# GLA scores in two row halves of the TensorE array, two heads each, into two PSUM banks

## The chip, the cores and the metric

One core of a Trainium2 chip runs the kernel. The metric is the device time of one execution in microseconds (us); the time before is the median of three runs. The engines are TensorE (PE, with its weight loads shown apart as PEld), VectorE (DVE), ScalarE (ACT), GpSimd (POOL) and SyncE (SP), which issues most of the DMAs.

## The reference, cut to what matters

Two layers of a backbone over 1024 latent tokens and 256 context tokens of width 1024. Each layer normalises and modulates the tokens, projects them, and gives the columns to four mixers (gated linear attention, neighbourhood attention, S5, pooling); their gated outputs are projected back and added. The change lies in the gated linear attention (GLA): four heads with keys and queries of 32 elements and values of 64, run forward and backward over the tokens.

```python
def step(state, inp):
    qc, kc, vc, gc = inp
    b = jnp.cumsum(gc, axis=-2)
    diff = b[:, :, :, None, :] - b[:, :, None, :, :]
    decay = jnp.exp(jnp.where(lower[:, :, None], diff, -jnp.inf))
    att = jnp.einsum('bhid,bhjd,bhijd->bhij', qc, kc, decay)
    o = (jnp.einsum('bhij,bhje->bhie', att, vc)
         + jnp.einsum('bhid,bhde->bhie', qc * jnp.exp(b), state))
    ...
o = (gla_chunked(qh, kh, vh, log_gate(gf, 0), s_f)
     + flip_seq(gla_chunked(flip_seq(qh), flip_seq(kh), flip_seq(vh), flip_seq(log_gate(gb, 1)), s_b)))
y = gla_head_norm(o, g_norm)
```

## The kernel before, in words

All 1280 tokens are cut into ten chunks of 128. Keys and queries of the four heads lie on the 128 partitions (32 per head), tokens along the free axis: QF and KF for the forward direction, QB and KB for the backward one, already multiplied with the exponentials of the gates.

A layer goes through stages: the GLA projections, then a stage in which GLA runs beside the projections of S5 and of the neighbourhood attention and beside the modulation, then S5, pooling, the neighbourhood attention and the output projection. `gla` (L978) is the GLA stage. Its preparation (`gla_prep`, L864, and L986 to L1012) makes the gates' running sums by scans, the four operands (L1002 to L1006), and a maximum over the gates (L1008), which PE transposes (L1010) and VectorE reduces to a flag; the flag chooses a general path, not taken here. A backward loop (L1049) builds the states of the backward direction for all chunks into `glSb`.

The forward loop (L1053 to L1073) then takes the chunks in order. For each chunk that is kept (ten in layer 0; eight in layer 1, where the context gives no output) and each direction:

- `gla_spread` copies the chunk's queries four times, each copy with the rows of one head kept and the others zero, into `qs` (128 x 512): by four ScalarE instructions (L971) forward, by one GpSimd instruction (L973) backward, as the string BD says.
- One fp32 matmul (L1062) with the keys as weights on all 128 rows and `qs` as the moving operand gives the scores of four heads, 128 x 512, in one PSUM bank of the pool `pb`.
- VectorE masks them into `at`: the forward direction by a multiplication (L1065), the backward one by a predicated copy over it (L1067). There are two `at` buffers (ATB).

`gla_finish` then sums into a `pb` bank: the forward state (L946, weights QF, moving operand `Sft`, made by VectorE at L1040), the masked scores times the values (L948, four heads), the backward state (L950). ScalarE squares the sums (L953), VectorE reduces the squares (L955), takes the reciprocal root in eleven small steps (L132 to L140) and multiplies (L957), PE transposes the result (L960), ScalarE writes `glyst` (L962) and it is stored. The forward state moves on by `state`: a transpose of the keys (L934), a copy by ScalarE (L936), a matmul (L938), two VectorE instructions (L1031, L1032).

PSUM in this stage: two banks for the projections (`pa`), one for the modulation (`pm`), five for GLA (`pb`; npb, L1536).

The order of instructions on every engine is set when the program is built, by a scheduler that takes GLA's instructions first and fills the gaps that it expects with the other mixers' projections (L318 with 512 columns, L334 with 256 columns, both into `pa`; their sums go on to `stn` and `stg` by L1200 and L1219 on VectorE) and with the modulation (L198 on 32 columns of the array, L229). Each engine then runs its list strictly in that order. In the trace an fp32 matmul of GLA appears as two instructions of the same columns.

## Time and profile before

| what | value |
|---|---|
| median of three runs | 1439.78 us (1434.55 to 1441.52) |
| the profiled execution's own time | 1441.78 us |
| its span | 1440.0 us |
| PE busy | 1286.8 us (89%) |
| DVE busy | 898.0 us (62%) |
| ACT busy | 585.0 us (41%) |
| POOL busy | 414.0 us (29%) |

The profile comes from one execution. The shares of busy time are means over stages with different limits, so the stretches and the waits in them tell more than the table.

### The profile page before, as it was taken

To read this page: it belongs to the slowest core of one execution; us is meant where nothing else is said; L and a number is where in the kernel's file an instruction comes from. 1 tells how busy PE (TensorE), PEld (TensorE's weight loads), DVE (VectorE), ACT (ScalarE), POOL (GpSimd) and SP (SyncE) were. 2 spreads that over 40 slices of the span, in tenths; PEclk is the share of its full clock that TensorE was granted. 3 is DMA by queue.
4 is the path that set the end of the run, shared out by engine and by line. 5 is a ranking of instruction groups with operands and counts; after the bars stand their busy time and mean duration, and the time that the engine had idled before them with its cause. 6 is when DMAs were issued, how large, how long until landed. Compare 5 with 4: busy or idle time off the path is not lost. (4 is left out here: it accounts for less than half of the span.)

```text
span 1440.0 us, 20173 instructions
## 1 busy us (share of the span) xinstructions
PE 1286.8 (89%) x6958; PEld 1025.7 (71%) x6958; DVE 898.0 (62%) x2113; ACT 585.0 (41%) x1218; POOL 414.0 (29%) x368
## 2 busy tenths in 40 slices
PE   5798988999999899989999898888989989977897
PEld 2687956567777688767778877856867766765676
DVE  2878576555378557844654578385553894776473
ACT  2642433222333346733455642442233323665321
POOL 0215342010101033432654536331121110234351
PEclk9798999999999999989999998989999999988999
DMA  9445674762533277726842374655324535755662
GB/s 333 144 125 182 210 214 137 211 178 64 178 116 115 91 202 179 208 87 210 241 130 92 113 215 163 205 169 143 107 77 158 156 125 150 196 158 163 180 205 90
DMA packets 223479, 231.09 MB, mean 160 GB/s; under 512 B 47016, under 2 KB 176552, under 8 KB 223040
## 3 DMA queue, kind: packets, MB, share of 16 engines
q1 hardware_dynamic: 221776, 227.14, 52.3%
q10 hardware_dynamic: 1584, 2.49, 0.5%
q8 instruction: 59, 0.97, 0.3%
q14 instruction: 60, 0.49, 0.1%
HBM read 159.97 MB, written 69.62 MB: 159 GB/s over the span
## 5 line engine op out<-in xcount | busy, mean ns | idle before, releaser
L303 POOL TENSOR_TENSOR wl<-w,wh 128x1024 fp32r<-128x1024 f32 (+1 forms) x45 | 118.1, 2632 | 437.6 <-PE pa L318 197.1
L318 PE MATMUL pa<-ahi,wh 128*128 128x512 f32 (+1 forms) x664 | 175.2, 392 | 5.5 <-DVE stg L856 2.5
L318 PE MATMUL pa<-ahi,wl 128*128 128x512 f32 (+1 forms) x664 | 171.1, 385 | 0.4 <-PEq L1555 0.4
L318 PE MATMUL pa<-alo,wh 128*128 128x512 f32 (+1 forms) x664 | 168.2, 380 | 0.1
L318 PEld LDWEIGHTS pa<-ahi,wh 128*128 128x128 f32 x664 | 119.2, 198 | 34.5 <-issue 8.4
L318 PEld LDWEIGHTS pa<-ahi,wl 128*128 128x128 f32 x664 | 117.1, 195 | 28.9 <-issue 11.3
L318 PEld LDWEIGHTS pa<-alo,wh 128*128 128x128 f32 x664 | 115.8, 194 | 25.5 <-issue 7.5
L334 PE MATMUL pa<-wh,ahi 128*128 128x256 f32 (+1 forms) x480 | 84.8, 311 | 6.3 <-ACT wh L302 2.4
L388 PE MATMUL po<-wx,ahi 128*128 128x512 f32 x312 | 82.8, 407 | 4.8 <-ACT ahi L380 2.6
L334 PE MATMUL pa<-wl,ahi 128*128 128x256 f32 (+1 forms) x480 | 81.5, 304 | 2.5 <-POOL wl L303 2.5
L334 PEld LDWEIGHTS pa<-wh,ahi 128*128 128x128 f32 x480 | 70.2, 201 | 14.2 <-issue 5.4
L334 PE MATMUL pa<-wh,alo 128*128 128x256 f32 (+1 forms) x480 | 78.2, 300 | 0.0
L302 ACT CAST wh<-w 128x1024 fp32r<-128x1024 f32 (+1 forms) x51 | 53.7, 1056 | 57.3 <-PE pa L318 34.9
L1315 PE MATMUL nS<-naK,naQ 128*128 128x256 f32 (+2 forms) x256 | 58.8, 349 | 19.8 <-DVE nast L1322 17.3
L388 PEld LDWEIGHTS po<-wx,ahi 128*128 128x128 f32 x312 | 61.1, 197 | 19.5 <-ACT ahi L380 3.5
L334 PEld LDWEIGHTS pa<-wl,ahi 128*128 128x128 f32 x480 | 69.2, 199 | 5.8 <-POOL wl L303 3.0
L334 PEld LDWEIGHTS pa<-wh,alo 128*128 128x128 f32 x480 | 67.9, 197 | 1.7 <-issue 1.4
L1322 DVE CUSTOM_DVE_ANT_0 naP<-nS,nab 128x640 f32<-128x640 f32 (+1 forms) x64 | 50.2, 785 | 28.9 <-ACT nab L1273 14.8
L1315 PEld LDWEIGHTS nS<-naK,naQ 128*128 128x128 f32 x256 | 45.0, 204 | 32.0 <-DVE nast L1322 26.2
L198 PE MATMUL pm<-wm,csil 128*32 128x512 f32 x192 | 47.8, 679 | 19.0 <-DVE nr2v L132 9.5
L973 POOL TENSOR_TENSOR qs<-QB,ind 128x512 f32<-128x512 f32 x18 | 18.8, 1047 | 148.4 <-PE pb L1062 144.3
L1327 ACT ACTIVATE naP<-naP,nast 128x640 f32<-128x640 f32 (+1 forms) x64 | 51.5, 804 | 22.8 <-DVE nast L1322 17.5
(395 smaller groups left out, 2735.2 us busy)
## 6 DMA issues: line engine op xcount, KB each, us to landing
wm<-in_w_mod_dram SPq DMA_DIRECT2D x48, 512.0 KB
w<-in_w_in_dram SPq DMA_DIRECT2D x41, 512.0 KB
s5R<-dR SPq DMA_DIRECT2D x16, 960.0 KB
xt<-in_tok_dram SPq DMA_DIRECT2D x20, 512.0 KB
dR<-sp_R SPq DMA_DIRECT2D x16, 512.0 KB
dG<-stg SPq DMA_DIRECT2D x32, 256.0 KB
w<-in_w_out_dram SPq DMA_DIRECT2D x16, 512.0 KB
naQ<-dQ SPq DMA_DIRECT2D x24, 320.0 KB
```

The source lines that it names most:

```text
L198: nc.tensor.matmul(state[0][32 * k:32 * k + 32, :], lhsT=self.csil[:, (k0 + k) // 2, 2 * (k % 2):2 * (k % 2) + 32], rhs=ws[k // 2][:, k % ...
L302: nc.scalar.copy(hi, raw)
L303: (next(engines) if engines else self.eng(2)).tensor_tensor(lo, raw, hi.bitcast(F32), ALU.subtract)
L318: nc.tensor.matmul(ps[:, :t1 - t0], lhsT=w(k), rhs=x[:, k, t0:t1], start=(i == 0), stop=(i == 23))
L334: nc.tensor.matmul(ps[:, :n], lhsT=x[:, k, t * 128:(t + 1) * 128], rhs=w(k), start=(i == 0), stop=(i == 23))
L388: self.nc.tensor.matmul(o, lhsT=x[:, k], rhs=m(k), start=first and i == 0, stop=last and i == len(todo) - 1)
L973: (nc.gpsimd if BD[d] == "p" else nc.vector).tensor_tensor(out, Q.unsqueeze(1).to_broadcast(sh), ind.unsqueeze(2).to_broadcast(sh), ALU.mult)
L1315: nc.tensor.matmul(ps[:, c * 128:(c + n) * 128], lhsT=Qb[:, i, :], rhs=K[:, b * 128:(b + n) * 128], start=(i == 0), stop=(i == 1))
L1322: v.tensor_tensor_reduce(P[:, 0:nk], ps, bias[:, b0:b0 + nk], 1.0, -NEG, ALU.add, ALU.min, nm)
L1327: nc.scalar.activation(P[:, 0:nk], src, AF.Exp, bias=nm, scale=-1.0, accum_out=l1)
```

## The change

The queries are spread to even and odd heads only. One copy keeps the rows of heads 0 and 2, the other those of heads 1 and 3 (`ind1` becomes 128 x 2), so `qs` has 128 x 256 elements; ScalarE makes both copies in both directions. The scores of a direction come from two matmuls: rows 0 to 63 of keys and `qs` (heads 0 and 1), and rows 64 to 127 (heads 2 and 3), 256 columns each. The two halves write into two PSUM banks: one tile `sc` of 1024 columns holds both directions of both halves of a chunk, and there is one such tile. The masks read it through a four-dimensional view. The pool `pb` goes from five banks to three.

```diff
--- before.py
+++ after.py
@@ -48,7 +48,6 @@
 WO = 0
 PO = ((4, 4, 'naK'), (0, 2, 'naQ'))
 OE = -2
-BD = 'ap'
 ATB = 2
 QSB = 2
 SLO = '11111111'
@@ -962,15 +961,10 @@
         nc.scalar.activation(yst, pt[:, 0:256].rearrange("p (m i) -> p m i", m=2), AF.Copy, scale=gn)
         self.q(1).dma_start(self.dY[l][0:256, c * 128:(c + 1) * 128].rearrange("(m p) i -> p m i", p=128), yst)
 
-    def gla_spread(self, out, Q, ind, d):
-
-        nc = self.nc
-        sh = [128, 4, 128]
-        if BD[d] == "a":
-            for h in range(4):
-                nc.scalar.activation(out[:, h], Q, AF.Copy, scale=ind[:, h:h + 1])
-        else:
-            (nc.gpsimd if BD[d] == "p" else nc.vector).tensor_tensor(out, Q.unsqueeze(1).to_broadcast(sh), ind.unsqueeze(2).to_broadcast(sh), ALU.mult)
+    def gla_spread(self, out, Q, ind):
+
+        for h in range(2):
+            self.nc.scalar.activation(out[:, h], Q, AF.Copy, scale=ind[:, h:h + 1])
 
     BWD = [1, 0] + list(range(NT - 1, 1, -1))
 
@@ -1015,7 +1009,7 @@
                 bm, gn = self.gla_consts(l)
                 mf = self.t([128, 128], "mF", 1)
                 nc.sync.dma_start(mf, a["maskF"])
-                ind = self.t([128, 4], "ind1", 1)
+                ind = self.t([128, 2], "ind1", 1)
                 nc.sync.dma_start(ind, a["ind1"])
                 mb = self.t([128, 128], "mB", 1, dtype=I32)
                 nc.sync.dma_start(mb, a["maskB"])
@@ -1054,17 +1048,21 @@
                     vt = self.gla_load_v(l, c)
                     if not (last and c < 2):
                         at = self.t([128, 4, 128], "at", ATB)
-                        sh = [128, 4, 128]
+
+                        ps = self.ps2.tile([128, 1024], F32, tag="sc", bufs=1, name=self.nm("sc"))
+                        pd = ps.rearrange("p (b d n) -> p d b n", b=2, d=2)
                         for d, (K, Q) in enumerate(((KF, QF), (KB, QB))):
-                            qs = self.t(sh, "qs", QSB)
-                            self.gla_spread(qs, Q[:, cs], ind, d)
-                            ps = self.pb()
-                            nc.tensor.matmul(ps, lhsT=K[:, cs], rhs=qs.rearrange("p h i -> p (h i)"), start=True, stop=True)
-                            pv = ps.rearrange("p (h i) -> p h i", h=4)
-                            if d == 0:
-                                v.tensor_tensor(at, pv, mf.unsqueeze(1).to_broadcast(sh), ALU.mult)
-                            else:
-                                v.copy_predicated(at, mb.unsqueeze(1).to_broadcast(sh), pv)
+                            qs = self.t([128, 2, 128], "qs", QSB)
+                            self.gla_spread(qs, Q[:, cs], ind)
+                            for b in range(2):
+                                hp = slice(64 * b, 64 * b + 64)
+                                nc.tensor.matmul(pd[:, d, b], lhsT=K[hp, cs], rhs=qs[hp].rearrange("p h i -> p (h i)"), start=True, stop=True)
+                        av = at.rearrange("p (b h) i -> p b h i", b=2)
+                        sh = [128, 2, 2, 128]
+                        every = lambda m: m.unsqueeze(1).unsqueeze(1).to_broadcast(sh)
+                        pv = pd.rearrange("p d b (h i) -> p d b h i", h=2)
+                        v.tensor_tensor(av, pv[:, 0], every(mf), ALU.mult)
+                        v.copy_predicated(av, every(mb), pv[:, 1])
                         sf = turned(S, 0, c, self.t([128, 256], "Sft", 2))
                         self.gla_finish(l, c, vt, lambda h: at[:, h, :], QF[:, cs], sf, QB[:, cs], Sb[:, c, :], gn)
                     if c != NT - 1:
@@ -1533,7 +1531,7 @@
                 psum = self.ps2
                 pm = lambda: psum.tile([128, 512], F32, tag="pm", bufs=1, name=self.nm("pm"))
                 todo = ((1, (2,)),) if last else ((0, (2,)), (1, (1, 0)))
-                self.npb = 5
+                self.npb = 3
                 flag = self.gla(l, last)
                 self.npb = 6
                 raws = itertools.cycle([("wm", 3, pool)])
@@ -1612,7 +1610,7 @@
     for h in range(4):
         ind[32 * h:32 * h + 32, h] = 2.0
     out["ind2"] = ind
-    out["ind1"] = (ind > 0).astype(f)
+    out["ind1"] = (ind[:, 0:2] + ind[:, 2:4] > 0).astype(f)
     lm = np.zeros((128, 5, 32), np.int32)
     j = np.arange(128)[:, None] % 32
     i = np.arange(32)[None]
```

Three lines come out of the changed file, so its numbers are lower: the score matmuls are L1059, L946, L948, L950, L955, L957 and L960 are L945, L947, L949, L954, L956 and L959, the masks are L1064 and L1065, L1040 is L1034, L1008 and L1010 are L1002 and L1004, L996 and L997 are L990 and L991, L1002, L1005 and L1006 are L996, L999 and L1000, L1031 and L1032 are L1025 and L1026, L318 and L334 are L317 and L333, L1200 and L1219 are L1198 and L1217.

The scheduler gives the instructions other places. PE, forward loop of layer 0, from the scores of one chunk to the transposes of another, before (`pa` is a projection's bank, `wh` and `wl` its weights, `ahi` and `alo` its tokens):

```order
L1062 MATMUL pb_2080<-qs_2075,KF_1561 128x512
L1062 MATMUL pb_2085<-qs_2083,KB_1563 128x512
L334 MATMUL pa_3328<-wh_3210,ahi 128x256 x3
L946 MATMUL pb_2090<-Sft_2088,QF_1560 128x256
L334 MATMUL pa_3328<-wl_3205,ahi 128x256 x2
L948 MATMUL pb_2090<-vt_2072,at_2074 128x64 x4
L950 MATMUL pb_2090<-glSb_1717,QB_1562 128x256
...
L334 MATMUL pa_3360<-wl_3205,ahi 128x256 x4
L334 MATMUL pa_3360<-wl_3211,ahi 128x256 x4
L960 MATMUL pb_2116<-c_ident,sq_2097 128x128 x2
```

The same place after, for a chunk of the same loop:

```order
L945 MATMUL pb_2150<-Sft_2148,QF_1560 128x256
L947 MATMUL pb_2150<-vt_2132,at_2134 128x64 x4
L949 MATMUL pb_2150<-glSb_1717,QB_1562 128x256
L333 MATMUL pa_3328<-wl_3211,ahi 128x256 x3
L333 MATMUL pa_3328<-wh_3204,alo 128x256 x4
L333 MATMUL pa_3328<-wh_3210,alo 128x256 x3
L1059 MATMUL sc_2315<-qs_2316,KF_1561 128x256 x2
L1059 MATMUL sc_2315<-qs_2321,KB_1563 128x256 x2
L333 MATMUL pa_3328<-wh_3210,alo 128x256
L333 MATMUL pa_3360<-wh_3204,ahi 128x256 x4
L333 MATMUL pa_3360<-wh_3210,ahi 128x256 x3
L959 MATMUL pb_2176<-c_ident,sq_2157 128x128 x2
```

The scores stood ahead of the sums of the same chunk; now they stand between the sums of one chunk (L947, L949) and its transposes (L959), and belong to a chunk three further on.

VectorE, the same loop, from the state to the norm, before (`at` is the masked scores, `gss` the norm's sum of squares):

```order
L1032 SCALAR_TENSOR_TENSOR S_494_2068<-S_474_2008,glsm_1564,km_2069 128x256
L1065 TENSOR_TENSOR at_2074<-pb_2080,mF_1711 128x512
L1040 TENSOR_SCALAR Sft_2088<-S_494_2068,glsm_1564 128x256
L1067 COPY_PREDICATED at_2074<-mB_1715,pb_2085 128x512
L955 TENSOR_REDUCE gss_2099<-sq_2097 128x4
```

And after:

```order
L1026 SCALAR_TENSOR_TENSOR S_490_2068<-S_471_2008,glsm_1564,km_2069 128x256
L1034 TENSOR_SCALAR Sft_2088<-S_490_2068,glsm_1564 128x256
L1064 TENSOR_TENSOR at_2194<-sc_2195,mF_1711 128x512
L1065 COPY_PREDICATED at_2194<-mB_1715,sc_2195 128x512
L1217 TENSOR_TENSOR stg_3286<-pa_3261,stg_3286 128x4x64
L954 TENSOR_REDUCE gss_2099<-sq_2097 128x4
```

The masks before belong to the chunk whose sums follow (`at_2074`); those after belong to a chunk two further on (`at_2194`), whose buffer is the one that L947 of this chunk reads (`at_2074`), so they run after that and ahead of the norm.

VectorE, layer 1's preparation, before (`glrg` holds the gates' ranges, `glmx` their maximum):

```order
L996 TENSOR_TENSOR glrg_12104<-glRB_12001 128x10
L997 TENSOR_TENSOR glrg_12104<-glRB_12001 128x10
L1002 TENSOR_SCALAR QB_11992<-QB_11992 128x1280
L1005 TENSOR_TENSOR KF_11991<-KF_11991,glk_11998 128x1280
L1006 TENSOR_TENSOR QF_11990<-QF_11990,glq_11999 128x1280
L1005 TENSOR_TENSOR KB_11993<-KB_11993,glk_11998 128x1280
L1200 TENSOR_TENSOR stn_13328<-pa_13303,stn_13328 128x8x8x8
L1006 TENSOR_TENSOR QB_11992<-QB_11992,glq_11999 128x1280
L1008 TENSOR_REDUCE glmx_12127<-glrg_12104 128x1
```

And after:

```order
L990 TENSOR_TENSOR glrg_12104<-glRB_12001 128x10
L991 TENSOR_TENSOR glrg_12104<-glRB_12001 128x10
L1002 TENSOR_REDUCE glmx_12127<-glrg_12104 128x1
L996 TENSOR_SCALAR QB_11992<-QB_11992 128x1280
L1006 TENSOR_REDUCE glm_2572_12131<-pb_12129 1x1
L999 TENSOR_TENSOR KF_11991<-KF_11991,glk_11998 128x1280
```

The maximum has moved from behind the multiplications of keys and queries to right behind its last input.

## Rows read from the trace of the kernel before

**Rows 1.** Busy time by stretches: us, then PE, PEld, DVE, ACT, POOL, PEclk, DMA share, GB/s.

```profile
260.00:280.00 20.00, 20.00 (x94) 11.21 (x91) 9.64 (x36) 4.01 (x11) 1.39 (x2) 1.00 0.71 215
...
1260.00:1280.00 20.00, 14.37 (x90) 12.13 (x89) 14.09 (x35) 11.63 (x27) 5.01 (x8) 0.88 0.67 180
1280.00:1300.00 20.00, 16.72 (x99) 14.06 (x99) 16.95 (x43) 12.93 (x30) 6.90 (x10) 0.87 0.55 152
```

**Rows 2.** Tile `sq` on PE: the transposes, and idle us, times, by releaser.

```profile
L960 PE MATMUL pb<-c_ident,sq x36: 271/273/331, 268.0 to 1091.5; 128*128 128x128 f32 x36
...
  DVE sq L957: 7.7, 11
```

**Rows 3.** Line 1062, its instructions: ns min/median/max, first and last start, form.

```profile
L1062 PE MATMUL pb<-qs,KF x36: 592/592/761, 257.3 to 1083.6; 128*128 128x512 f32 x36
```

**Rows 4.** Timeline of PE, first scores: start us, us, line, operation, count.

```profile
257.29 1.02 PE L1062 MATMUL pb<-qs,KF 128*128 128x512 f32 x2
258.15 1.02 PE L1062 MATMUL pb<-qs,KB 128*128 128x512 f32 x2
259.01 0.59 PE L946 MATMUL pb<-Sft,QF 128*128 128x256 f32 x2
```

**Rows 5.** Timeline of PE around one row of the modulation (L198).

```profile
246.31 0.63 PE L318 MATMUL pa<-ahi,wl 128*128 128x256 f32 x4
246.87 1.05 PE L198 MATMUL pm<-wm,csil 128*32 128x512 f32 x4
247.85 0.74 PE L318 MATMUL pa<-ahi,wl 128*128 128x256 f32 x4
248.44 0.39 PE L318 MATMUL pa<-ahi,wh 128*128 128x512 f32 x1
```

**Rows 6.** Timeline of PE, projections of 512 columns, layer 1.

```profile
960.99 1.98 PE L318 MATMUL pa<-ahi,wh 128*128 128x512 f32 x8
962.80 1.98 PE L318 MATMUL pa<-alo,wh 128*128 128x512 f32 x8
```

**Rows 7.** Timeline of PE, S5's output stage, into transposes on 64 rows.

```profile
477.78 1.03 PE L822 MATMUL pb<-s5g,s5wg 128*128 128x256 f32 x4
478.74 0.71 PE L810 MATMUL pb<-c_ident,s5yc 64*128 64x64 f32 x8
```

**Rows 8.** Timelines of PE and VectorE, one chunk's sums and norm, layer 1.

```profile
1052.39 1.00 PE L948 MATMUL pb<-vt,at 128*128 128x64 f32 x8
1053.23 0.65 PE L950 MATMUL pb<-glSb,QB 128*128 128x256 f32 x2
...
1057.52 0.44 PE L960 MATMUL pb<-c_ident,sq 128*128 128x128 f32 x2 [0.20 <-DVE sq L957]
...
1050.55 0.68 DVE L1065 TENSOR_TENSOR at<-pb,mF 128x512 f32<-128x512 f32 x1
...
1051.41 0.74 DVE L1067 COPY_PREDICATED at<-mB,pb 128x512 f32<-128x512 int32 x1
...
1054.33 0.42 DVE L955 TENSOR_REDUCE gss<-sq 128x4 f32<-128x256 f32 x1 [2.18 <-ACT sq L953]
```

**Rows 9.** Timelines of PE and VectorE, layer 0's maximum and a projection's addition.

```profile
223.22 0.27 PE L1010 MATMUL pb<-c_ident,glmx 128*1 128x128 f32 x1 [4.66 <-DVE glmx L1008]
...
225.60 0.69 DVE L1200 TENSOR_TENSOR stn<-pa,stn 128x512 fp32r<-128x512 f32 x1
```

**Rows 10.** Timelines of VectorE and PE, layer 1's maximum.

```profile
968.59 0.17 DVE L997 TENSOR_TENSOR glrg<-glRB 128x10 f32<-128x10 f32 x1
...
975.62 0.18 DVE L1008 TENSOR_REDUCE glmx<-glrg 128x1 f32<-128x40 f32 x1
...
975.86 0.37 PE L1010 MATMUL pb<-c_ident,glmx 128*1 128x128 f32 x1 [4.36 <-DVE glmx L1008]
```

**Rows 11.** Timeline of PE, the last projection of layer 1.

```profile
1263.48 0.47 PE L318 MATMUL pa<-ahi,wl 128*128 128x512 f32 x1
```

## The prediction

> **What bounds the kernel now.** I read the busy time by stretches first, then the groups of the lines that are edited, then the timelines of TensorE (PE) and VectorE (DVE) around them. In the middle of layer 0's GLA loop PE is busy for 20.00 of 20 us, VectorE for 9.64, ScalarE for 4.01, GpSimd for 1.39 [rows 1]: projections of other mixers fill every gap, so time taken from PE there, and idle time brought in there, both count. The exception is one short wait: after a chunk's sums are normalised on VectorE, PE transposes them at L960, and it sat idle there 11 times for 7.7 us in all [rows 2]. VectorE is never the bound by its busy time, only by the length of that chain.
>
> **Part 1, the scores themselves (PE).** The 36 score matmuls have 512 columns each [rows 3], and follow each other at 257.29, 258.15 and 259.01, so 0.86 us apiece [rows 4]: 36 x 0.86 = 31.0 us. After, each becomes two of 256 columns on half of the rows, 0.43 each by the same pitch. If two halves run side by side, a neighbouring pair takes 0.43. By the order, 12 of the 18 chunks have their four halves together (2 x 0.43 = 0.86), layer 0's chunk 0 has four single ones (1.72), four chunks have two single ones and a pair (1.29 each), layer 1's chunk 0 one and then three (1.29). That is 10.3 + 1.7 + 5.2 + 1.3 = 18.5 us. That row halves run side by side no row shows; column groups do: the four instructions of L198 take from 246.87 to 247.85, 0.98, where the same columns one after the other would take 2 x 0.86 = 1.72 [rows 4, 5].
>
> Leaving the full array has a price. A projection instruction of 512 columns takes (962.80 - 960.99)/8 = 0.226 [rows 6], one of 256 columns half, 0.113. So the four ahead of L198 should end at 246.31 + 0.45 = 246.76, and L198 starts at 246.87: 0.11. L198 takes 0.98 and not 0.86: 0.12. The four behind it take 0.59 (247.85 to 248.44) and not 0.45: 0.14 [rows 5]. Together 0.37 per excursion. Going to the 64-row shape of L810 costs 478.74 - (477.78 + 4 x 0.215) = 0.10 [rows 7], the same as going to L198, so I take 0.37. The score halves leave the full shape 30 times (12 x 1 + 4 + 4 x 3 + 2): 11.1 us. **Part 1: 18.5 + 11.1 - 31.0 = -1.4 us**; bounds -12.5 (no price, halves side by side) and +11.1 (price, halves one after the other).
>
> The Trainium skill, "TensorE: Matmul & The Clock Gate" (Part 3: Packing small matmuls), gives for matmuls on different rows a span of one matmul plus some 4 ns for each further one, and names no price for leaving the full shape; by it part 1 would be -12.5. "TensorEngine Tiling (Array Packing)" (Overview, Key Properties) of the same skill says that a change of the mode drains TensorE; the trace agrees, with the 0.37 us just read around L198. That speaks against this change.
>
> **Part 2, the chain that PE waits for (PE, VectorE).** This term is the largest. There is one score tile now, so the scores of chunk c+1 wait until both masks of chunk c have read it; those need a buffer `at` that L948 of chunk c-2 frees. Before, both masks were done ahead of L948, and the norm began when ScalarE had squared the sums. In the new order both masks stand behind L948 and in front of the norm's reduction. Before: L950 starts at 1053.23, the reduction L955 at 1054.33 (1.10 later), the transposes L960 at 1057.52 after a wait of 0.20, so the chain is 4.29 us from L950's start [rows 8]. After: L948 ends at 1052.39 + 1.00 = 1053.39, 0.16 past L950's start; the two masks stand 0.86 apart and the second takes 0.74 [rows 8]; with 0.06 for a hand-over from one engine to another (L1008's end at 975.80 to L1010's start at 975.86 [rows 10]) they end 1.8 after L950's start, 0.7 later than the reduction starts now. The chain becomes 4.99.
>
> Against it stands what PE has to do from L950 to L960. Counted from the order with the prices above (0.43 for L950, 0.226 or 0.113 per projection instruction, 0.215 per one of L198, 0.43 per score pair, 0.37 per excursion, 0.11 for each of the small rest): before, 4.52 4.73 4.27 4.18 3.82 3.92 3.48 4.26 3.48 3.82 in layer 0 and 3.82 3.82 3.48 3.82 3.82 2.46 3.82 3.82 in layer 1. What is short of 4.29 adds up to 8.5 us, against the 7.7 measured [rows 2], so the count holds to a tenth. After, the twelve windows with masks and scores in them have 4.62 4.04 4.49 4.80 4.03 3.69 4.02 and 3.92 4.03 3.92 3.69 4.03: short of 4.99 by 10.6. The last three chunks of each layer have no masks left ahead: 5.06 3.48 3.03 and 4.38 3.82 3.03, short of 4.29 by 3.8. **Part 2: 14.4 - 8.5 = +5.9 us.** The wait of the next scores for the masks lies inside the same windows and isn't counted again (the masks end 1.8 after L950's start, and PE's own work from there to the scores is 1.6 to 2.3). Bounds: 0, if the masks still come before the sums, and +14.3, if the chain grows by twice as much.
>
> **Part 3, layer 0's preparation.** PE waits 4.66 us at L1010 (223.22) for VectorE's maximum [rows 9]. In the new order 17 projection matmuls of 256 and 4 of 512 columns have moved ahead of L1010 into that wait, 17 x 0.113 + 4 x 0.226 = 2.8 us, and one more addition of a projection, 0.69 [rows 9], stands ahead of the maximum on VectorE: **-2.8 + 0.7 = -2.1**. Bounds 0 and -2.8.
>
> **Part 4, layer 1's preparation.** The maximum L1008 runs at 975.62, behind the multiplications of K and Q; its last input is done at 968.59 + 0.17 [rows 10]. In the new order it stands right behind that input, so it comes 975.62 - 968.76 = 6.9 us earlier. But 41 of the 512-column projection matmuls (9.3 us) have moved from ahead of L1010 to behind it, so PE's wait there grows from 4.36 [rows 10] by 9.3 - 6.9 = 2.4. Of these, by the order, 24 (5.4 us) are carried beyond the GLA and S5 stages, well into the neighbourhood attention, where today the projections run out at 1263.48 [rows 11] and PE is busy 14.37 and 16.72 of 20 us (5.6 + 3.3 idle) [rows 1]. There they take idle time: **+2.4 - 5.4 = -3.0**. Bounds +2.4 (nothing fits) and -6.9 (the carried work costs nothing).
>
> **At nothing.** GpSimd loses 18 multiplications; it is busy 1.39 of 20 us there [rows 1], and PE waits for nothing of it. ScalarE keeps its 72 spreads (18 chunks with four heads in one direction, now with two in both); it has 16 of 20 us free [rows 1]. The masks keep their 512 columns. The PSUM pool of three buffers instead of five carries four allocations per chunk instead of six; each buffer's reader is done before the third next asks for it, by the order, so no wait of its own.
>
> **Sum.** -1.4 + 5.9 - 2.1 - 3.0 = -0.6 us. The profiled execution took 1441.78, so 1441.2; it stands 2.0 above the median of the three runs, so against the median 1439.78 the forecast is 1439.2, **1439 us**. A measurement of this kernel can tell about 0.5% (7.2 us) from no change; this is inside.
>
> **The rivals.**
> Packing pays in full: no price for the excursions. For: at L198 the price is of column groups of 32, and the halves here use all columns. Against: L810's 64-row shape has an entry cost of 0.10 [rows 7]. It gains 11.1, but in the twelve windows 12 x 0.37 = 4.4 of it become wait for the same chain: 1439.2 - 6.7 = 1432.5. "TensorE: Matmul & The Clock Gate" (Part 3) of the Trainium skill, by its span without a switching price, speaks for this case.
> The halves run one after the other: +12.5, but in the twelve windows PE then has 0.86 more to do and 8.8 of the wait vanish: 1443. For: no row shows fp32 row halves together. Against: column groups do run together.
> The idle time of parts 3 and 4 isn't recovered (another wait comes next, or the fillers land where PE is full): +5.1, so 1444. For: what is late after L1010 is the state loop, which needs the same VectorE.
> Slower: the mask chain is longer than I reckon. Place: VectorE between L948 and L957. If one more projection addition (0.69) stands in it, or the masks on two banks take 0.35 longer each, each of the twelve windows grows by 0.7: +8.4, so 1447.6; with two additions, 1456. It decides from 0.7 us per window ((1447.0 - 1439.2)/12 = 0.65). For: VectorE runs strictly in its order, and a sum's addition already falls between the norm's steps now and then. Against: it is 48% busy there [rows 1].
>
> **Chances.** Forecast 0.34, packing in full 0.24, idle time not recovered 0.16, halves one after the other 0.08, longer mask chain 0.18. The forecast's own spread is 1434 to 1444. Faster by over 0.5% (under 1432.6): three quarters of the packing case, with gains of parts 3 and 4 towards their bounds, and a small part of the forecast, 0.23. Slower by over 0.5% (over 1447.0): two thirds of the longer chain and a part of the unrecovered case with it, 0.17. Within: 0.60. The range from 1429 to 1448 takes in the packing case with 3 us to spare below, and the longer chain's price; about 2 in 10 lie outside.
>
> **What would show it.** Score halves: two starts within some 0.05 us and the pair in 0.43 confirms side by side, a pitch of 0.43 refutes it; the matmul behind them late by some 0.1 shows the price. L960 should wait for L957 about 14 us in all (7.7 now) with the reduction some 1.8 after L950's start. L1010's wait should be near 2.5 in layer 0, and 6.8 in layer 1, the latter with the maximum near 969. The stretch 1260 to 1300 should show PE over 5 us busier. I am wrong if L960's wait stays at 7 or less, if PE's idle time appears in front of the score matmuls by more than 3 us in all, or if the median leaves 1429 to 1448.

## The result, and the profile after

The change makes the kernel slower: 1448.53 us in the median of eight runs (1442.31 to 1455.69) against 1439.82 of eight runs of the kernel before beside it; ratio 1.0056, 95% interval 1.0032 to 1.0080. That is 8.7 us by the medians, and 0.5 us above the upper end of the forecast range. Run twice more, it gave 1.0068 and 1.0020; the medians of these, 1447.71 and 1442.37, lie inside the range, so that the first lies just outside it is in part chance. The profiled execution took 1445.53 us (span 1443.7), 3.0 below its median and 3.75 above the profiled execution of before; the sums below are made between these two, and show less than half of the loss.

Part 1 of the page of the kernel after, busy time by engine, to be held against the table of before:

```profile
PE 1279.6 (89%) x7030; PEld 1028.2 (71%) x7030; DVE 905.5 (63%) x2113; ACT 585.9 (41%) x1218; POOL 394.0 (27%) x350
```

PE is busy for 7.2 us less than before and the kernel is longer: what was taken from PE came back as idle time. Where, tells a table of the span cut at events of PE (first or last starts of the named lines of before; in after they are 1 to 6 less, the scores L1059 for L1062). Lengths are in us, idle is the length less PE's busy time in that stretch; the last column has the lengths in three profiles of the changed kernel.

| from, to | before: length, idle | after: length, idle | after, three profiles |
|---|---|---|---|
| layer 0: first gate product L901 to L1010 | 61.1, 10.5 | 68.4, 15.3 | 68.4 to 68.5 |
| L1010 to the last L960 (GLA loops) | 146.7, 5.0 | 140.3, 6.5 | 138.1 to 142.9 |
| last L960 to the first attention scores L1315 (S5) | 147.3, 8.2 | 151.8, 8.6 | 150.1 to 151.8 |
| L1315 to the first output projection L388 | 145.9, 12.0 | 143.8, 12.0 | 140.2 to 143.8 |
| L388 to layer 1's first L274 (seam) | 48.7, 2.9 | 54.4, 6.8 | 50.6 to 54.4 |
| L274 to layer 1's first L901 | 190.0, 20.5 | 192.7, 19.9 | 190.5 to 193.5 |
| first L901 to L1010 | 74.0, 12.1 | 62.5, 12.5 | 62.5 to 63.4 |
| L1010 to the last L960 | 115.6, 5.5 | 116.0, 6.9 | 115.4 to 116.0 |
| last L960 to L1315 (S5) | 130.8, 8.5 | 141.2, 14.1 | 141.2 to 144.9 |
| L1315 to the last L388 | 208.9, 28.6 | 201.9, 23.2 | 201.8 to 203.6 |

The GLA loops, for which the change was made, are not where it loses: layer 0's are shorter, layer 1's the same. PE's idle time grows by 12 us: 4.8 in layer 0's preparation, 2.9 in the two loops, 3.9 at the seam, 5.6 in layer 1's S5, with 5.4 won back in the last attention. In S5 and at the seam the edit touches nothing but the order of the work. A length is no loss by itself, as projection matmuls have moved between the stages: layer 0's loops have 36 fewer of L317, of which 21 stand ahead of them now and 15 in S5.

**Scores.** Timeline of PE after; a single pair of half scores, then four halves together:

```profile
246.81 0.64 PE L317 MATMUL pa<-alo,wh 128*128 128x256 f32 x4
247.38 0.70 PE L1059 MATMUL sc<-qs,KF 64*128 64x256 f32 x2
248.01 0.70 PE L937 MATMUL pb<-vt,kt 128*128 128x256 f32 x2
...
1027.66 0.99 PE L333 MATMUL pa<-wh,ahi 128*128 128x256 f32 x7
1028.58 0.70 PE L1059 MATMUL sc<-qs,KF 64*128 64x256 f32 x4
1029.12 0.60 PE L1059 MATMUL sc<-qs,KB 64*128 64x256 f32 x4
1029.65 0.39 PE L333 MATMUL pa<-wh,ahi 128*128 128x256 f32 x1
1029.87 1.12 PE L333 MATMUL pa<-wl,ahi 128*128 128x256 f32 x8
```

The four score instructions of one direction (two halves, two instructions each) take 1029.12 - 1028.58 = 0.54, where one after the other they would take 0.86; cut at 1028.62, the same view has two of them begun already, while the two instructions of a single half begin 0.32 apart (247.38 and 247.70). So the halves do run side by side. Both directions take 1.07 to the next projection, where before they took 1.72 [rows 4]. A half alone takes 0.63 (247.38 to 248.01) and not 0.43.

The price of leaving the full shape shows in full: 1027.66 + 7 x 0.113 = 1028.45, so entry costs 0.13; 1.07 exceeds 2 x 0.43 by 0.21; and the projection behind takes 0.22 (1029.65 to 1029.87) and not 0.113, 0.11 more. Together that is 0.45 per excursion, where 0.37 was reckoned. "TensorEngine Tiling (Array Packing)" of the Trainium skill (Tiling Modes, Key Properties) has a drain at a change of mode, and these rows agree. The packing span in "TensorE: Matmul & The Clock Gate" of the Trainium skill (Part 3: Packing small matmuls), without such a price, fits the side-by-side starts and not the 1.07.

**The chain to the transposes.** Tile `sq` on PE after (answers to [rows 2]), then the timelines of PE and VectorE of one chunk (answers to [rows 8]):

```profile
L959 PE MATMUL pb<-c_ident,sq x36: 270/273/329, 271.4 to 1091.9; 128*128 128x128 f32 x36
...
  DVE sq L956: 9.7, 16
```

```profile
1025.98 1.00 PE L947 MATMUL pb<-vt,at 128*128 128x64 f32 x8
1026.82 0.65 PE L949 MATMUL pb<-glSb,QB 128*128 128x256 f32 x2
...
1031.82 0.44 PE L959 MATMUL pb<-c_ident,sq 128*128 128x128 f32 x2 [0.59 <-DVE sq L956]
...
1027.02 0.69 DVE L1064 TENSOR_TENSOR at<-sc,mF 128x512 f32<-128x512 f32 x1 [1.69 <-PE pb L947]
1027.74 0.76 DVE L1065 COPY_PREDICATED at<-mB,sc 128x512 f32<-128x512 int32 x1
...
1028.72 0.41 DVE L954 TENSOR_REDUCE gss<-sq 128x4 f32<-128x256 f32 x1
```

The masks stand where the order put them, right behind L947, and the reduction begins 1.9 us after L949 (forecast 1.8). The transposes follow L949 by 5.00 (forecast 4.99). The sum of waits is 9.7 us, not 14.4.

**Layer 0's and layer 1's preparation.** Timelines of PE and VectorE after (answer to [rows 9, 10]):

```profile
192.60 0.72 DVE L892 STREAM_SHUFFLE QF<-glk 128x512 f32<-128x512 f32 x1
...
202.38 0.46 DVE L902 TENSOR_SCALAR QF<-pb,bg 128x256 f32<-128x256 f32 x1
...
202.90 0.58 PE L900 MATMUL pb<-glgT,wg 128*128 128x256 f32 x1 [4.58 <-DVE QF L902]
...
230.35 0.37 PE L1004 MATMUL pb<-c_ident,glmx 128*1 128x128 f32 x1 [6.43 <-DVE glmx L1002]
...
975.59 0.20 DVE L1002 TENSOR_REDUCE glmx<-glrg 128x1 f32<-128x40 f32 x1
...
975.84 0.37 PE L1004 MATMUL pb<-c_ident,glmx 128*1 128x128 f32 x1 [5.12 <-DVE glmx L1002]
```

The same place before, timeline of VectorE:

```profile
187.75 0.73 DVE L893 STREAM_SHUFFLE QF<-glk 128x512 f32<-128x512 f32 x1
```

With three banks a gate matmul (L900) waits 4.58 us for VectorE to read an earlier gate product; before, with five, PE had no such wait in layer 0. In layer 1 it had one of 3.54 already (L901 at 941.17), which is 6.88 now (L900 at 950.23). In layer 0 VectorE's first shuffle comes 4.9 us later, and the maximum's transpose waits 6.43 and starts 7.1 later than [rows 9] has it.

**S5 of layer 1 and the attention.** Busy time by stretches after (columns as in [rows 1]), and under it two of the same stretches before:

```profile
1120.00:1180.00 60.00, 52.34 (x273) 41.27 (x272) 55.01 (x91) 20.40 (x42) 8.31 (x4) 1.00 0.50 160
1180.00:1236.00 56.00, 50.51 (x220) 36.40 (x219) 27.55 (x43) 17.66 (x28) 4.88 (x4) 0.95 0.39 117
1191.00:1195.00 4.00, 3.75 (x15) 2.71 (x15) 1.92 (x5) 0.87 (x2) 0.00 (x0) 0.70 0.65 214
1260.00:1280.00 20.00, 19.65 (x130) 16.75 (x129) 17.51 (x45) 13.74 (x34) 3.45 (x5) 1.00 0.73 190
1280.00:1300.00 20.00, 16.14 (x93) 13.64 (x92) 15.72 (x38) 13.31 (x28) 9.57 (x12) 0.91 0.69 194
```

```profile
1120.00:1180.00 60.00, 54.82 (x287) 42.72 (x287) 53.73 (x93) 21.86 (x46) 8.26 (x3) 1.00 0.49 160
1180.00:1236.00 56.00, 54.24 (x262) 40.06 (x261) 33.04 (x64) 23.91 (x42) 7.23 (x8) 1.00 0.54 146
```

From 1260 to 1300 PE is busy 4.7 us more than in [rows 1]: the carried projections do fill idle time there (the last now runs near 1286, not 1263 [rows 11]). But from 1120 to 1236 it is busy 6.2 us less. By the count of projection matmuls in the two stages of the table, S5 has 366 (349 before) and the attention 79 (61): 17 and 18 more, 3.8 and 4.1 us by the pitch of [rows 6]. So of S5's 10.4 us some 3.8 are carried work and 5.6 idle time. Timelines of VectorE, GpSimd and PE after, and the waits of PE from 1095 to 1236 (line waited for, us in total, times, longest), of after and then of before:

```profile
1188.57 2.35 POOL L302 TENSOR_TENSOR wl<-w,wh 128x1024 fp32r<-128x1024 f32 x1 [16.51 <-PE pa L317]
1188.61 2.59 DVE L778 TENSOR_TENSOR s5x<-s5v,s5x 64x256 f32<-64x256 f32 x1
...
1191.72 0.42 DVE L778 TENSOR_TENSOR s5x<-s5v,s5x 64x256 f32<-64x256 f32 x1
...
1191.25 0.49 PE L788 MATMUL pb<-s5R,s5x 128*128 128x128 f32 x2 [2.37 <-DVE s5x L778]
```

```profile
PE pb L788 <- DVE s5x L778: 8.3, 4, 2.4
```

```profile
PE pb L789 <- DVE s5x L779: 4.8, 4, 1.5
```

One VectorE instruction took 2.59 us where another of the same form takes 0.42; it began with GpSimd's L302 (the low part `wl` of a projection's weights) and ended just behind it. The stage has five VectorE steps that are so much longer than others of their form, 10.5 us in all, and each stands beside an L302; before there were four, 6.6 us. PE's list had no projection ahead of the matmul that waited for it (L788), and behind that wait the granted clock is 0.70 for 4 us. A longer S5 is no loss by itself, though: sc_prep5 (below), as fast as before, has 142.1 us with 13.6 idle there.

**The seam.** PE's timeline, its busy time after, and then GpSimd's waits from 640 to 722 after and before:

```profile
712.27 6.66 PE L387 MATMUL po<-wx,ahi 128*128 128x512 f32 x16 [3.62 <-DVE stg L473]
718.77 2.01 PE L387 MATMUL po<-wx,alo 128*128 128x512 f32 x8
```

```profile
712.30:719.00 6.70, 6.70 (x18) 5.27 (x18) 4.35 (x17) 3.40 (x7) 4.95 (x5) 0.56 0.65 197
719.00:722.00 3.00, 3.00 (x18) 2.48 (x17) 2.93 (x7) 1.63 (x2) 1.62 (x2) 1.00 0.93 269
```

```profile
POOL yt L377 <- DMA gt<-dG: 22.7, 7, 8.0
```

```profile
POOL yt L378 <- DMA gt<-dG: 15.0, 4, 7.4
```

PE idled 3.62 us, and the next 16 matmuls took 6.50 where the pitch of [rows 6] gives 3.6: the clock stood at 0.56 of full speed, mostly the lower of its two levels (1.2 of 2.4 GHz), and went back to 1.00. The idle time is lost, and 2.9 us more. This place varies with the execution: the stretch took 54.4, 50.6 and 54.0 us in three profiles of the same kernel, and GpSimd waited 22.7, 16.8 and 20.1 us. The 15.0 of the kernel before, of which there is one profile, is the least among all eighteen profiles; the versions of it that are tried below have 16.6 to 20.2. So part of the 5.6 us is no property of the change.

### The profile page after: what moved, and what is told of

Its sections match the earlier page's. It is cut to its first block, busy times and chain, and to the rows that moved or that the text cites. A ratio compares the mean times of both kernels' runs of the same rounds, so it can differ in the third digit from the quotient of the medians.

```text
span 1443.7 us, 20276 instructions
## 1 busy us (share of the span) xinstructions
PE 1279.6 (89%) x7030; PEld 1028.2 (71%) x7030; DVE 905.5 (63%) x2113; ACT 585.9 (41%) x1218; POOL 394.0 (27%) x350
## 5 line engine op out<-in xcount | busy, mean ns | idle before, releaser
L302 POOL TENSOR_TENSOR wl<-w,wh 128x1024 fp32r<-128x1024 f32 (+1 forms) x45 | 116.0, 2585 | 607.6 <-ACT wh L301 253.0
L317 PE MATMUL pa<-ahi,wh 128*128 128x512 f32 (+1 forms) x664 | 170.8, 387 | 6.8 <-DVE stg L855 2.5
L317 PE MATMUL pa<-ahi,wl 128*128 128x512 f32 (+1 forms) x664 | 169.5, 384 | 0.4 <-PEq L1553 0.4
L317 PE MATMUL pa<-alo,wh 128*128 128x512 f32 (+1 forms) x664 | 168.7, 383 | 0.1
L317 PEld LDWEIGHTS pa<-ahi,wh 128*128 128x128 f32 x664 | 116.9, 196 | 35.2 <-issue 8.4
L317 PEld LDWEIGHTS pa<-alo,wh 128*128 128x128 f32 x664 | 117.7, 195 | 27.6 <-issue 9.2
L317 PEld LDWEIGHTS pa<-ahi,wl 128*128 128x128 f32 x664 | 118.3, 196 | 25.1 <-issue 6.6
L333 PE MATMUL pa<-wh,ahi 128*128 128x256 f32 (+1 forms) x480 | 85.2, 313 | 7.7 <-DVE gates L845 2.9
L333 PE MATMUL pa<-wl,ahi 128*128 128x256 f32 (+1 forms) x480 | 80.9, 304 | 2.5 <-POOL wl L302 2.5
L333 PEld LDWEIGHTS pa<-wh,ahi 128*128 128x128 f32 x480 | 71.8, 206 | 14.2 <-issue 4.7
L333 PE MATMUL pa<-wh,alo 128*128 128x256 f32 (+1 forms) x480 | 79.5, 304 | 0.0
L333 PEld LDWEIGHTS pa<-wl,ahi 128*128 128x128 f32 x480 | 69.8, 201 | 3.9 <-POOL wl L302 2.9
L333 PEld LDWEIGHTS pa<-wh,alo 128*128 128x128 f32 x480 | 69.3, 202 | 1.1 <-issue 0.7
L1313 PEld LDWEIGHTS nS<-naK,naQ 128*128 128x128 f32 x256 | 44.1, 200 | 27.0 <-DVE nast L1320 20.1
L474 POOL TENSOR_TENSOR xt<-xt,stg 128x512 f32<-128x512 f32 x34 | 45.4, 1356 | 46.8 <-DVE stg L473 35.4
L1365 DVE TENSOR_TENSOR naPT<-nT,naPT 128x512 fp32r<-128x512 f32 (+2 forms) x104 | 56.0, 559 | 3.0 <-ACT naPT L1364 2.3
```

What stands on the lines that cost most here:

```text
L302: (next(engines) if engines else self.eng(2)).tensor_tensor(lo, raw, hi.bitcast(F32), ALU.subtract)
L317: nc.tensor.matmul(ps[:, :t1 - t0], lhsT=w(k), rhs=x[:, k, t0:t1], start=(i == 0), stop=(i == 23))
L333: nc.tensor.matmul(ps[:, :n], lhsT=x[:, k, t * 128:(t + 1) * 128], rhs=w(k), start=(i == 0), stop=(i == 23))
L474: self.eng(5).tensor_tensor(xt[:, hs], xt[:, hs], ob, ALU.add)
L1313: nc.tensor.matmul(ps[:, c * 128:(c + n) * 128], lhsT=Qb[:, i, :], rhs=K[:, b * 128:(b + n) * 128], start=(i == 0), stop=(i == 1))
L1365: (nc.gpsimd if RLO == "p" and len(src) < 4 else nc.vector).tensor_tensor(lo, pv, hi.bitcast(F32), ALU.subtract)
```

## The experiments

The theories: the wait moved, because of the one score tile in the loop (theory A) or of three banks in the preparation (theory B); the row groups cost by themselves (theory C); the order of the instructions decides (theory O, against theory P, by which the parts do), as the scheduler rearranges everything when tiles, banks or costs change. The edits are cut to the lines that matter. Ratios are to runs of the kernel before on the same chip, with 95% intervals.

### Parts of the change alone

**before_pb3**: the kernel before with three banks.

```diff
-                self.npb = 5
+                self.npb = 3
```

> The kernel before with the PSUM pool pb cut from five banks to three and nothing else: scores as before (four heads, 512 columns, one matmul on all rows), two banks unused. By its order it has the changed kernel's preparation (2.8 us more of projections ahead of the maximum in layer 0, 9.2 us fewer in layer 1), but the filler of the loop as before (203.2 us at the last transposes of layer 0, 499.6 in layer 1). Theory A (the time is lost in the chunk loop, by the one score tile): no slower than before, 0 to -5 us, the gain of parts 3 and 4. Theory B (the time is lost in the preparation, because the gate matmuls L901 wait for one of only three banks; in the changed kernel the layer 0 maximum came 7.1 us later): +6 to +9 us, with L901 waiting some 4.6 us for L902 in layer 0. Theory C (the price of leaving the full array shape is larger than 0.37): 0.

Measured 1.0103 (1.0071 to 1.0135), 1453.47 us, 14.4 above before: more than any of the three theories had. L901 waits 4.0 us for L903 in layer 0, as theory B has it. By the medians three banks for six tiles per chunk are 5.8 us worse than the whole change on the same chip (1447.71), though the intervals overlap.

**before_sc**: three banks, and one 1024-column score tile; scores stay whole (512 columns, four heads).

```diff
-                            ps = self.pb()
-                            nc.tensor.matmul(ps, lhsT=K[:, cs], ...)
+                        ps = self.ps2.tile([128, 1024], F32, tag="sc", bufs=1, ...)
+                            nc.tensor.matmul(pd[:, d], lhsT=K[:, cs], ...)
```

> The kernel before with the changed kernel's PSUM plan: one score tile of two banks for both directions of a chunk, one buffer, pool of three banks, both masks after both scores; the scores themselves as before (one matmul of 512 columns on all rows, spread to four heads by ScalarE and GpSimd). Its order carries the projections behind the loop as the changed kernel does (199.8 us at the last transposes of layer 0 against 203.2, 491.8 in layer 1 against 499.6). Theory A: slower than before by 6 to 10 us, as much as the changed kernel, since packing itself gives 1.4 us at most. Theory B: the same time as the run with three banks alone, +6 to +9. Theory C: no slower than before, since the array never leaves the full shape in the scores.

Measured 1.0032 (1.0005 to 1.0058), 1445.17 us: slower, against theory C, and by the ratio (4.6 us) less than theories A and B have.

**after_pb5**: the row halves with five banks; the two halves take two `pb` banks, with four masks of 256 columns.

```diff
-                        ps = self.ps2.tile([128, 1024], F32, tag="sc", bufs=1, ...)
+                        pb = [self.pb() for b in range(2)]
...
-                self.npb = 3
+                self.npb = 5
```

> The changed kernel's packed scores in the PSUM plan of before: each half of the rows writes both directions into a bank of its own out of the five of pb, so masks are four of 256 columns instead of two of 512. By its order all 18 chunks have their four halves together (18 excursions, not 30), and preparation and filler stand as before. Streaming 18 x 0.86 = 15.5 and 18 x 0.37 = 6.7 for the excursions, against 31.0: -8.8 us on TensorE, of which the norm's chain may take some back (masks longer by some 0.4 us a chunk). Theory A and theory B: faster than before by 4 to 9 us, about 1433. Theory C: the packing costs more than it gives, slower than before by 4 us or more.

Measured 1.0027 (1.0003 to 1.0051), 1442.21 us. By size that is next to theory C (slower by 4 us or more), but the next run, before_split, is as slow without the halves. The packing is no gain here. Timelines of PE and VectorE of after_pb5, and PE's waits: from 1000 to 1100, of after_pb5 and then of before, and from 255 to 380, of after_pb5 and then of before_split (the same banks and masks, with the scores on all rows):

```profile
1030.74 0.70 PE L1059 MATMUL pb<-qs,KF 64*128 64x256 f32 x4
1031.27 0.60 PE L1059 MATMUL pb<-qs,KB 64*128 64x256 f32 x4
1032.39 0.67 PE L945 MATMUL pb<-Sft,QF 128*128 128x256 f32 x2 [0.52 <-DVE Sft L1034]
...
1030.85 0.48 DVE L1025 SCALAR_TENSOR_TENSOR km<-pb,glsm,bmask 128x256 f32<-128x256 f32 x1 [1.95 <-PE pb L937]
1031.88 0.35 DVE L1034 TENSOR_SCALAR Sft<-S,glsm 128x256 f32<-128x256 f32 x1
```

```profile
PE pb L945 <- DVE Sft L1034: 3.5, 7, 0.5
```

```profile
PE pb L946 <- DVE Sft L1040: 0.2, 1, 0.2
```

```profile
PE pb L945 <- DVE Sft L1034: 5.9, 8, 2.2
```

```profile
PE pb L946 <- DVE Sft L1040: 1.5, 1, 1.5
```

The score matmuls used to cover the three VectorE steps from `km` to `Sft`; shortened to 1.07, they no longer do, and PE waits 0.5 us a chunk for `Sft`. Over the whole run that is 9.4 us in 15 waits, against one of 1.5 in before_split: where the gain of the halves goes in this order.

**before_split**: the kernel before, each direction's scores in two matmuls of 256 columns on all rows, same banks and masks as after_pb5.

```diff
+                            for b in range(2):
+                                nc.tensor.matmul(pd[b][:, d], lhsT=K[:, cs], rhs=qs[:, 2*b:2*b+2]...)
```

> The kernel before with each direction's scores in two matmuls of 256 columns, still on all 128 rows and with four-head spreads, into two banks out of five, and four masks of 256 columns: the order of the packed run with five banks, without the row groups. Streams 18 x 1.72 = 31.0 us as before, no excursions. If the masks' cut is what made packing in five banks slow (four masks of 0.38 to 0.40 us and their starts against two of 0.68 and 0.73), this is as slow as that run, +3 to +5 us; if the row groups themselves cost (excursions, or waits that they uncover), this is as fast as before, 0 to +1, and the packed run 3 us slower than it; if packing gave its 8.8 us and something else ate them, this would be +10 or more.

Measured 1.0030 (1.0007 to 1.0052), 1442.82 us: the same as after_pb5 (two chips). So the masks' cut, or the order that comes with it, costs the 0.3%, and row halves against all rows make no difference here.

**before_pb4**: `self.npb = 4` in the kernel before.

> The kernel before with four banks in the pool instead of five, nothing else. By its order it differs from before in the preparation and hardly from the run with three banks (127.7 us of projections ahead of the layer 0 maximum, against 127.6 with three banks and 124.8 with five). Theory B, the late gate matmuls by their place in the order: about the +14.4 us of three banks, +10 to +15, with L1010 of layer 0 near 230. If it is the waits for a bank at run time that cost, one of them fewer: +3 to +8.

Measured 1.0008 (0.9984 to 1.0033), 1442.61 us, against both expectations. Its L1010 in layer 0 comes 9.4 us later than before (7.1 in the kernel after). Layer 0 as a whole is 9 us longer, and layer 1 is 7.2 us shorter than before (the table under "The sum"); its profiled execution, at 1447.66, is 5 us above its median.

### With and without row groups in nearly the same order

**sc_split**: the kernel after without row groups: scores in 256-column matmuls on all rows, spreads of four heads. On PE 40 of 8346 matmuls stand elsewhere than in the kernel after.

```diff
-                                nc.tensor.matmul(..., lhsT=K[hp, cs], rhs=qs[hp]...)
+                                nc.tensor.matmul(..., lhsT=K[:, cs], rhs=qs[:, 2*b:2*b+2]...)
```

> The changed kernel without row groups: one score tile, three banks, four matmuls of 256 columns a chunk into the same two banks and the same two masks, but each matmul on all 128 rows with four-head spreads (ScalarE forward, GpSimd backward). Its order of matmuls is the changed kernel's but for 40 of 8346. Streams 31.0 us of scores instead of 18.5, with no excursions (11.1). If the row groups themselves cost (excursions of more than 0.37 us, weights that load no more behind a matmul), this is faster than the changed kernel by 3 to 6 us, 1442 to 1445. If they are worth nothing either way and the order is what counts: within 2 us of the changed kernel, 1446 to 1450. If packing gave something: slower than it.

Measured 1.0078 (1.0047 to 1.0109), 1450.49 us. The change itself, on the same chip, gave 1.0020 (1442.37 us, 8.1 less, and the intervals don't meet); on others it gave 1.0056 and 1.0068. So the halves gave something here, 0.1 to 0.6%, the most of it on the same chip.

**after_prep5, sc_prep5, sc_split_prep5**: the kernel after, before_sc and sc_split, with two of the preparation's gate products per six put into the score tile's idle banks, so that three banks no longer hold them up.

```diff
+                    if self.npb == 3 and d == 0 and i == 1:
+                        two = self.ps2.tile([128, 1024], F32, tag="sc", bufs=1, ...)
-                    ps = self.pb()
+                    ps = two[:, 512*i-512:512*i] if self.npb == 3 and d == 0 and i else self.pb()
```

> The changed kernel, but in the preparation two of the six gate matmuls (L901) of a layer write into the two banks of the score tile, which lies idle there, so five banks serve the preparation as before; the chunk loop keeps its three banks and its score tile. Theory B (the time is lost in the preparation for want of banks): L1010 of layer 0 back at 223 us (230 in the changed kernel), and most of what the changed kernel lost is given back: 1437 to 1441 us. Rival D (three banks cost in the loop and in what is carried behind it): no gain over the changed kernel, 1446 to 1450, though L1010 comes earlier.

> The same two banks for the preparation, with the scores of before (512 columns on all rows, four heads) in the one score tile. Theory B: 1435 to 1439 us, under before, by the 7 us of layer 0's preparation against the 1445.2 of the run without them. Rival D: 1444 to 1447. Against after_prep5 it gives the cost of packing a second time: the changed kernel stood 2.5 us above the same plan with unpacked scores, so after_prep5 should be 2 to 5 us slower than this.

> The run with five banks for the preparation and packed scores, without row groups: matmuls of 256 columns on all rows, the same order but for 53 of 8346. The packed one took 1457.8, the one with 512-column scores 1439.5, and their orders differ in 265 matmuls. If the order of layer 1 is what cost the 18 us, this is as slow as the packed one, 1453 to 1460; if the row groups or ScalarE's spreads cost them, as fast as the other, 1437 to 1443.

Measured 1.0124 (1.0088 to 1.0160), 0.9988 (0.9969 to 1.0007) and 1.0153 (1.0118 to 1.0187). The edit did its work: first L901 to L1010 took 58.7, 61.9 and 58.8 us (68.4 in the kernel after, 61.1 before). It mended before_sc and made the change worse, so this wait alone does not decide. And sc_prep5 shows an order in which three banks, one score tile, and masks in front of the norm cost nothing. Against sc_split_prep5, with 53 matmuls elsewhere, the row groups are again 0.3% the faster. Over the three pairs they are worth 0 to 0.6%, and never a loss.

### The change again

> The changed kernel once more, for a second profile on this chip: 1445 to 1452 us. The first profile had 8.8 us more than before between 700 and 721 us, at the seam of the layers, where the multiplication with the gates waits for a load (gt), and nothing before it. If that is chance, this profile has another value there; if it is the change's doing, it is there again.

> The changed kernel a third time, on the same chip as the run without row groups, for that comparison: 1445 to 1451 us. Its profile shows whether the seam of the layers (700 to 721 us) is 8.8 us late, as in the first profile, or 2.6, as in the second; the order being the same, a third value would say that the loads there vary from execution to execution.

> The packed scores with five banks for the preparation once more, on the same chip as the run before: 1453 to 1461 us if the 18 us belong to the kernel. If they belonged to that chip or those executions: nearer to 1445.

The kernel after, unedited: 1.0068 (1.0044 to 1.0091) and 1.0020 (0.9996 to 1.0044); after_prep5, unedited: 1.0118 (1.0083 to 1.0152). The third is faster than was expected of it, and its interval takes in no change at all. By the three measurements the change costs 0.2 to 0.7%.

### Order alone

**before_swap**: the kernel before with the backward scores issued first, and both masks behind both scores. Every instruction, size and bank count stays.

```diff
-                        for d, (K, Q) in enumerate(((KF, QF), (KB, QB))):
+                        for d in (1, 0):
```

> The kernel before with the backward direction's scores computed ahead of the forward's, the masks as before: the same instructions on every engine, in another order (the scheduler draws 5.4 us more projections into layer 0's loop, 208.6 us at its last transposes against 203.2). Theory O (the order decides, whatever the parts cost): any value off by 5 us or more, either way. Theory P (the parts decide): within 3 us of before, as nothing is added.

Measured 1.0167 (1.0140 to 1.0194), 1462.62 us: more than any part of the change. Waits of PE over the whole run of before_swap; then its projection matmuls (L318, the count behind the first x) in S5 and in the attention of layer 1, and under them those of the attention before:

```profile
PE pb L946 <- DVE Sft L1040: 9.4, 14, 2.2
```

```profile
1094.06:1238.85 144.79, 100.49 (x373) 70.53 (x373) 0.95 0.44 143
1238.85:1448.19 209.34, 3.02 (x11) 1.81 (x10) 0.92 0.57 165
```

```profile
1222.31:1431.18 208.87, 19.23 (x61) 11.24 (x61) 0.93 0.59 171
```

At the first output projection of layer 0 it is 5.4 us ahead of before (657.7 against 663.1), so it loses nothing in layer 0, although `Sft` makes PE wait there (3.9 us in seven waits, 2.1 in one before). The whole loss stands in layer 1. Its loops take 123.1 us (115.6 before), with 5.5 us of waits for `Sft` (0.2 before), and S5 takes 144.8 (130.8 before). The order has moved work: some 50 projection matmuls that ran in the last attention before, 11 us of them, now stand in the loops (151, 124 before) and in S5 (373, 349 before). PE has little idle time to spare there, and in the attention, where they covered waits, it is idle for 37.9 us (28.6 before). So this run shows what an order can do, and part of how: by where it puts the fillers.

**sc_prep5_swap**: the same swap in sc_prep5.

> The run with 512-column scores in the one score tile and five banks for the preparation (ratio 0.9988), with the backward scores first: same instructions, filler by stages the same to 0.5 us. Its order lies between that run and the one with 256-column scores (ratio 1.0153). Theory O: may be off the 0.9988 by 0.005 or more. Theory P: 0.996 to 1.002.

Measured 1.0079 (1.0050 to 1.0108) against 0.9988 without it: the swap costs 0.9% there. Here each stage has the same number of projection matmuls as in sc_prep5 (127, 359 and 79 in layer 1's loops, S5 and attention), so this is the cleaner test of the order.

**after_bfirst, after_prep5_bfirst**: in the kernel after and in after_prep5, both directions of the lower half are issued ahead of the upper half.

```diff
-                        for d, (K, Q) in enumerate(((KF, QF), (KB, QB))):
+                        for b in range(2):
+                            for d in range(2):
```

> The changed kernel with the two directions of the lower half of the rows ahead of the two of the upper half: the halves that run side by side no longer stand next to each other in a direction, so where a chunk's four stand together only the second and third are on different rows: 3 x 0.43 = 1.29 us a chunk in place of 0.86, +0.43 x 12 = 5 us on TensorE, if side by side is what the halves gain from; the same filler by stages. Packing worth its overlap: +3 to +5 us against the changed kernel. Packing worth nothing, because what it frees becomes wait for VectorE: within 2 us of it.

> The same order of halves in the slow run with five banks for the preparation (ratios 1.0124 and 1.0118). Theory O: its order differs in the first chunks of both layers, so it may fall back towards 1.000 to 1.006. Theory P: 1.012 to 1.017, the three half matmuls in a row added.

Measured 1.0053 (1.0024 to 1.0082) and 1.0077 (1.0050 to 1.0104). Timeline of PE of after_bfirst:

```profile
1028.66 0.71 PE L1061 MATMUL sc<-qs,KF 64*128 64x256 f32 x4
1029.20 0.60 PE L1061 MATMUL sc<-qs,KB 64*128 64x256 f32 x4
1029.73 0.39 PE L333 MATMUL pa<-wh,ahi 128*128 128x256 f32 x1
```

A chunk still takes 1.07, so where all four halves stand together this edit did not take the overlap away, and it tests little but the order: by it after_prep5 gains about 0.4%, the kernel after nothing (each on another chip).

## Why the prediction was wrong

**Part 1, right.** The halves run side by side: a chunk's four take 0.86 + 0.45 = 1.31 with the price, against 0.86 + 0.37 = 1.23 reckoned and 1.72 before. A pair takes 0.54 and not 0.43. No idle time stands in front of a score matmul, as the prediction has it. Pairs of kernels in nearly the same order put the row groups at 0 to -0.6%; the forecast term was -1.4 us, 0.1%. The two rivals on the scores (packing paid in full, halves one after the other) are refuted by the 1.07.

**Part 2, mechanism right, size wrong.** +2.0 us measured (9.7 against 7.7), +5.9 reckoned. The chain's length was right (5.00 against 4.99), and waits came 16 times. PE's own work in the windows was put too low: the chunk shown has 5.00 less 0.59 of idle time, 4.41, where layer 1's windows with masks were reckoned at 3.69 to 4.03. The rival of a longer mask chain, the one that ended slower, did not happen; that the time is where it put it is chance.

**Part 3, wrong sign.** The step that failed is the sentence under "At nothing" that three banks bring no wait of their own. It was worked out for the allocations of a chunk; in the preparation, gate products hold the banks, and L900 waits 4.58 us. L1010's wait is 6.43 and not 2.5, and its stage 7.3 us longer. The loops behind it were 6.4 shorter, but with 36 projection matmuls fewer in them, so that gives nothing back. What the wait costs shows in the kernels with all-row scores: layer 0 up to its first L388 takes 7 to 9 us longer with three or four banks, and no longer in sc_prep5, where the wait is gone (first column of the table below; one profile each). In the changed kernel it is 3.3 and 0.9 us longer and 2.6 shorter in three profiles, so there most of the cost is not seen, and after_prep5, without the wait, gains nothing in layer 0.

**Part 4, half right.** From the first L901 to L1010 layer 1 takes 11.5 us less (forecast: 9.3 of matmuls moved out, 2.4 more wait); the wait at L1010 is 5.12, not 6.8. The maximum is at 975.59, not near 969, since all ahead of it had become some 11 us later. The carried projections do take idle time in the attention: 5.4 us less of it, as forecast. What failed is that 24 of them "are carried beyond the GLA and S5 stages" at no cost in between: of the 41 that left the preparation 18 came to the attention, 17 to S5 and 6 to the loops, and S5 itself lost 5.6 us to idle time, as PE's list had no projection ahead of the matmuls that waited for VectorE's `s5x`.

**The sum.** It listed the places at which the diff and the order named a wait, and priced every other moved instruction at nothing. The profiled execution shows +0.9 us for layer 0's preparation and loops together (forecast +0.4: part 3, and ten of 18 chunks of parts 1 and 2), -7.7 from layer 1's first L901 on (forecast -1.0), and +10.8 in between, where the forecast had nothing; of this 5.6 is the seam. That is one execution, below its median; in the median the loss is twice as large. Cut at three events, all profiles of a kernel side by side, the runs differ like this:

| us | layer 0: first L901 to first L388 | to layer 1's first L901 | to the last L388 | ratio |
|---|---|---|---|---|
| before | 501.0 | 238.8 | 529.3 | 1 |
| after | 504.3, 501.9, 498.4 | 247.1, 244.0, 244.5 | 521.7, 525.5, 526.5 | 1.0056, 1.0068, 1.0020 |
| before_pb3 | 508.2 | 240.4 | 528.1 | 1.0103 |
| before_pb4 | 510.0 | 241.2 | 522.1 | 1.0008 |
| before_sc | 508.7 | 241.2 | 524.6 | 1.0032 |
| sc_prep5 | 499.8 | 241.8 | 528.3 | 0.9988 |
| sc_split | 504.7 | 243.1 | 530.7 | 1.0078 |
| after_prep5 | 501.5, 504.6 | 245.2, 244.8 | 539.6, 536.6 | 1.0124, 1.0118 |
| before_swap | 496.0 | 240.5 | 549.9 | 1.0167 |

The three profiles of the changed kernel agree: layer 1 is shorter than before, as part 4 had it, layer 0 is the same on average, and the loss stands between the layers, where the edit touches nothing. There the kernel before has the lowest value of all eighteen profiles, so some of that difference is its one execution; the other runs in the table with whole scores have 240.4 to 241.8. The sum had no term for this stretch. That an order can take 7 to 21 us in layer 1, after_prep5 and before_swap show. The range, 10 us down and 9 up, allowed for unknown prices and not for this. That the change's 0.2 to 0.7% is an effect of order is argued from its parts (0.9988 for tile, banks and masks with the preparation's banks given back; 0 to -0.6% for row groups), not shown by a run that holds the order of before and has all the rest.

**Open.** Why the stretch between the layers is longer with the change is not shown: the eight profiles of kernels with row halves have 242.6 to 247.1 us there, the ten without 238.8 to 245.0. Why one order is 1 to 2% slower than another is shown by place, and for before_swap in part by the fillers that moved; for after_prep5 and sc_prep5_swap it stays open. No version ran clearly faster than the kernel before.

## What to carry to other kernels

Where a scheduler fills a busy engine's gaps, a change of tiles, banks or issue order rearranges the whole list. That alone cost 0.9% with as many fillers in every stage, and 1.7% where it also took fillers out of a stage that had idle time for them: count the fillers by stage, and compare an edit with a twin that has the same order, or its own small effect can't be seen. When matmul time is removed, look at what those matmuls covered on VectorE; in after_pb5 0.65 us less per chunk came back as 0.5 us of waiting for the state. And count PSUM banks in every stage that draws on the pool, not only in the loop that is edited.
